# Two layers of attention and experts on one core: pair 0's scores ahead of the other queries and the values, the best keys behind its maximum, and each gathered tile split between ACT and DVE

## The chip, the cores and the metric

The kernel runs on one core of a Trainium2 chip. The metric is the device time of one execution in microseconds. Before the change three runs took 1065.91, 1067.25 and 1068.90 us, with a median of 1067.25; a profiled execution of the same kernel took 1066.29.

## What is computed

The input x has 256 tokens of 1024 features, all in fp32. A first block (attention with a causal mask, a pooling mixer, gates, an FFN with a convolution) is not touched by the change. Then come two layers (`DEPTH_2 = 2`), each of which does this:

```python
mix = hybrid_mixer(x, ...)                  # MLA and DSA side by side, then w_o
x = layer_norm(ALPHA * x + mix, ...)
ffn = grouped_moe(x, ...)                   # 16 experts, 2 for each token
x = layer_norm(ALPHA * x + ffn, ...)
```

The mixer projects x once and hands the parts to two groups of 8 heads. MLA norms a query latent of 384 and a key latent of 256, multiplies them up to queries, keys and values, and does a causal softmax. DSA has an index that picks the keys:

```python
def mla_group(...):
    q = (rms_norm(qa, q_norm_g) @ w_q_up).reshape(B, T, 8, 64 + 32)   # 32 of them rotated
    c_kv = rms_norm(kva, kv_norm_g)
    k_nope, v = c_kv @ w_uk, c_kv @ w_uv
    p = softmax(causal(q k^T * scale));  out = p @ v

def dsa_group(...):
    score = sum_h relu(iq_h ik^T * 32 ** -0.5) * iw_h      # causal
    _, sel = lax.top_k(score, n_keep)                      # n_keep = 64 of 256 keys
    s = q k_sel^T * scale - slopes * dist;  out = softmax(s) @ v_sel
```

In the MoE each token goes to two of 16 experts (two from one group of four); each expert is silu(x w_gate) * (x w_up), weighted, times w_down.

## The kernel before

T is 256 tokens, in two tiles of 128. PE multiplies in fp32 by parts: a high and a low half of each operand, and three matmuls (`mm3`, L76). `split` (L96) makes the halves: ACT copies the high one, DVE subtracts for the low one (`lo_of`, L86). So the lines L74 (every matmul), L96 and L86 are helpers' lines, and the tile names tell what is what.

A scheduler orders the instructions of each engine, by priority in program order and by costs. An engine runs its list strictly in that order. `tc.issue_after(i)` adds an edge: what is issued within it comes after instruction i on the same engine. Buffers come from pools, and a buffer's release is a wait for whoever takes it next. PSUM has two: "A" (four tiles of one bank, [128, 512] fp32) and "H" (two tiles of two banks, [128, 2, 512], for the scores `sc`). Weights go through a ring in SBUF, and for the experts through the freed buffers of the attention too; SP issues their DMAs in order, and each waits for its buffer.

In `layer` the projections come first (`proj`), and between them `index_scores`, which adds up the index heads' scores in `score`, [128, 384]: queries 0 to 127 against 128 keys, queries 128 to 255 against 256 keys. Then:

- `latent_stats` (L952 to L955): sums of squares on PE, a square root on ACT, and on DVE the reciprocal `rn`.
- `keys`: PE multiplies `knp`; `key_row` (L960) transposes rn into `prk` on PE and DVE copies it (`at`, L961); DVE multiplies both into `kx` (L975).
- `queries(g)` for the four pairs of heads: splits of `qu`, 18 matmuls into `qp`, and DVE's product with the rotation into `qx` (L1001).
- `values_`: split of `uv`, 12 matmuls into `vps`, copied by ACT.
- `mla_pair(j)`, j = 0 to 3: scores `sc` from kx and qx, the causal mask, then `softmax_heads` (L385): DVE's maximum (L390, two instructions) and scale (L394), four exponentials on ACT (L397), DVE's reciprocal (L400) and product (L402) to the normalised `P`, six transposes on PE (L406), copied half by ACT (L409) and half by DVE (L411), the matmuls with the values, and the halves oh and ol.
- `best_keys` (L934 to L939): eight rounds, each with DVE's eight largest (`MAX`, L936) and a replacement of these in `score` (`MATCH_REPLACE`, L937), for both parts of `score`; then the mask `selm` (L938, L939).
- Projections 11 and 12, and `wo_prep`: splits of w_o, issued after `first`, the normalisation (L402) of pair 0.
- `dsa_pair(j)`: scores, slopes, `selm` as a mask matmul, `softmax_heads` again, and w_o.

In the expert part `gather(q)` (L1194) fetches the tokens of four experts by matmul: four tiles `pg` of one bank, [128, 2, 256], each holding two of the eight feature blocks. `affine` (L1101 on ACT, L1103 on DVE) applies the norm's gain and bias on the way to `xg`, which `gate_up` reads for `gu`. The tiles b = 0 and 2 leave by ACT, 1 and 3 by DVE. `gather(2)` and `gather(3)` stand among the copies of an earlier expert pair's output `y` (ACT's copy L1323, DVE's low half L86), which `combine` adds up into `sum`. The weight DMAs of the experts are issued by `Experts.pump` (L733 to L757).

Of the kernel before, what the change touches and what calls it, by code (L numbers as in the profile page):

```python
# [11 lines left out]
F32R = mybir.dt.float32r  # L12
# [3 lines left out]
ALU = mybir.AluOpType  # L16
AX = mybir.AxisListType
# [17 lines left out]
def body(tc, a, out, dbg=None, upto=None):  # L35
# [17 lines left out]
    def act(name, dt=F32, shape=(128, KD, T)):  # L53
        return wp.tile(list(shape), dt, tag="act", name=name, bufs=10)
# [330 lines left out]
    def softmax_heads(S, n_, scale, nscale, values, hi, lo):  # L385

        m = sm[:, n_ % 4].rearrange("p f (h t) -> p f h t", t=2)
        P, PT = (v[:, 0:768].rearrange("p (h c) -> p h c", h=2) for v in pair_of(pp8("P")))
        for tt, (c, n) in enumerate(SPAN):
            ve.tensor_reduce(out=m[:, 0, :, tt], in_=S[:, :, c:c + n], axis=AX.X, op=ALU.max)  # L390
        if isinstance(scale, float):
            ve.tensor_scalar(m[:, 1], m[:, 0], nscale, None, op0=ALU.mult)
        else:
            ve.tensor_tensor(out=m[:, 1], in0=m[:, 0], in1=nscale[:, None, :].to_broadcast([128, 2, 2]), op=ALU.mult)  # L394
        for tt, (c, n) in enumerate(SPAN):
            for i in range(2):
                se.activation(P[:, i, c:c + n], S[:, i, c:c + n], AF.Exp,  # L397
                              scale=scale if isinstance(scale, float) else scale[:, tt:tt + 1],
                              bias=m[:, 1, i, tt:tt + 1], accum_out=m[:, 2, i, tt:tt + 1])
        ve.reciprocal(m[:, 3], m[:, 2])  # L400
        for tt, (c, n) in enumerate(SPAN):
            done = ve.tensor_tensor(out=P[:, :, c:c + n], in0=P[:, :, c:c + n],  # L402
                                    in1=m[:, 3, :, tt:tt + 1].to_broadcast([128, 2, n]), op=ALU.mult)
        for i in range(2):
            for b in range(3):
                te.transpose(S[:, i, 128 * b:128 * b + 128], P[:, i, 128 * b:128 * b + 128], ident)  # L406
        for i in range(2):
            if i == 0:
                se.activation(PT[:, i], S[:, i, 0:384], AF.Copy)  # L409
            else:  # L410
                ve.tensor_copy(PT[:, i], S[:, i, 0:384])  # L411
        o = S[:, :, 384:512]
        for i in range(2):
            mm(o[64 * i:64 * i + 64, 0], values(0, i), PT[:, i, 0:128], True, True)
        for i in range(2):
            mm(o[64 * i:64 * i + 64, 1], values(0, i), PT[:, i, 128:256], True, False)
        for i in range(2):
            mm(o[64 * i:64 * i + 64, 1], values(1, i), PT[:, i, 256:384], False, True)
        hi, lo = (v.rearrange("p (t c) -> p t c", t=2) for v in (hi, lo))
        se.activation(hi, o, AF.Copy)  # L420
        lo_of(lo, o, hi)
        return done

    def causal(S):
        for i in range(2):
            for c in (0, 256):
                mm(S[:, i, c:c + 128], identb, at.maskb[:, c:c + 128], False, True)
# [371 lines left out]
    def layer(l, xT, xh, xl, general=False):  # L799
# [178 lines left out]
        def values_():  # L978
            uvh, uvl = split(W[f"uv{l}"].rearrange("p k f -> p (k f)"))
            for tt in range(2):  # L980
                ps = A("vps")
                for k in range(2):
                    c = slice(k * 512, k * 512 + 512)
                    t_ = slice(tt * 128, tt * 128 + 128)
                    mm(ps, nh[:, 3 + k, t_], uvh[:, c], k == 0, False)
                    mm(ps, nh[:, 3 + k, t_], uvl[:, c], False, False)
                    mm(ps, nl[:, 3 + k, t_], uvh[:, c], False, k == 1)
                se.activation(vm[:, tt], ps, AF.Copy, scale=rn[:, 2, 2 + tt:3 + tt])

        def queries(g):  # L990

            qu = W[f"qu{l}"].rearrange("p k (h c) -> p k h c", c=96)[:, :, 2 * g:2 * g + 2]
            hi, lo = (v.rearrange("p (k h) c -> p k h c", h=2) for v in split(None, (6, 128)))
            for d, c in ((slice(0, 96), slice(0, 96)), (slice(96, 128), slice(64, 96))):
                se.activation(hi[:, :, :, d], qu[:, :, :, c], AF.Copy)
                lo_of(lo[:, :, :, d], qu[:, :, :, c], hi[:, :, :, d])
            ps = A("qp", (128, 2, T))
            for i in range(2):
                for k in range(3):
                    mm3(ps[:, i], hi[:, k, i], lo[:, k, i], nh[:, k], nl[:, k], k == 0, k == 2)  # L1000
            ve.tensor_tensor(out=qx[:, 2 * g:2 * g + 2], in0=ps, in1=at.qrot[:, None, :].to_broadcast([128, 2, T]), op=ALU.mult)  # L1001

        def mla_pair(j):
            S = H("sc")
            for tt, (c, n) in enumerate(SPAN):
                for i in range(2):
                    h = 2 * j + i
                    mm(S[:, i, c:c + n], qx[:, h, tt * 128:tt * 128 + 128], kx[:, h, 0:n], tt == 0, False)
            causal(S)
            return softmax_heads(S, j, rn[:, 2], rn[:, 3, 0:2], lambda s, i: vm[:, s, (2 * j + i) * 64:(2 * j + i) * 64 + 64],  # L1010
                                 oh[:, j], ol[:, j])

# [22 lines left out]
        latent_stats()  # L1035
        keys()
        qx = act("qx")
        queries(0)
        queries(1)
        values_()  # L1040
        queries(2)
        queries(3)
        oh, ol = act("oh", F32R), act("ol", F32R)
        first = [mla_pair(j) for j in range(4)][0]
        best_keys()
        for i in range(11, 13):
            proj(i)
        if not general:
# [49 lines left out]
        def affine(dst, src, k, eng):  # L1098
            g, b = V(f"ln1g{l}", k), V(f"ln1b{l}", k)
            if eng is se:  # L1100
                se.activation(dst, src, AF.Identity, scale=g, bias=b)  # L1101
            else:
                ve.tensor_scalar(dst, src, g, b, op0=ALU.mult, op1=ALU.add)  # L1103
# [79 lines left out]
        def gather(q, bs=range(4)):  # L1183

            G = GS[q]
            if q not in XG:
                XG[q] = act("xg", shape=(128, KD, 256))
            xg = XG[q]
            for b in bs:
                pg = A("pg", (128, 2, 256))  # L1190
                for tt in range(2):
                    for i in range(2):
                        k = 2 * b + i
                        mm(pg[:, i], zh[:, tt, k], G[:, tt], tt == i == 0, False)  # L1194
                        mm(pg[:, i], zl[:, tt, k], G[:, tt], False, tt == 1)
                for i in range(2):
                    affine(xg[:, 2 * b + i], pg[:, i], 2 * b + i, (se, ve)[b % 2])

        def gate_up(p, m):
            ps = A("gu")  # L1200
# [305 lines left out]
```

## Time and profile before

| | |
|---|---|
| median of three runs | 1067.25 us (1065.91 to 1068.90) |
| the profiled execution | 1066.29 us |
| its span in the trace | 1064.2 us, mean granted clock 0.994 |
| PE busy | 1020.2 us, 96% |
| DVE / ACT / POOL busy | 50% / 40% / 7% |
| DMA | 278 GB/s over the span, 388 GB/s from 497 to 700 us |
| layer 0: attention and DSA / experts | about 397 to 470 us / 486 to 700 us |
| layer 1: MLA / experts | about 746 to 794 us / 848 to 1054 us |

The span runs from the first to the last instruction; the execution's own time adds 2.1 us around it. A row of the timeline has its start in us, its length, engine, line, operation, what is written and read, shapes and count, and in brackets the idle time before it with the instruction that ended it. A row of a window has the busy time and count of each engine, the granted clock of TensorE (1.00 is 2.4 GHz), the DMA share and GB/s.

### The profile page before, as it was taken

What the parts mean: (1) busy time and instruction counts of PE and PEld (TensorE: products, weight loads), DVE (VectorE), ACT (ScalarE), POOL (GpSimd) and SP (SyncE); (2) the same over time, 40 slices, a digit from 0 to 9 for tenths busy, and PEclk for the clock granted to TensorE, in tenths of its full rate; (3) what the DMA queues carried; (4) which work ended last, traced back from release to release, by engine and by line L of the source; (5) the groups of instructions that cost most, each with busy time, mean ns of one, the idle gap of its engine ahead of it and who ended that gap; (6) DMA issues with size and microseconds to landing.
All of it is one profiled execution on the core that took longest, in us unless ns stands there. A gap on an engine that the chain in (4) does not pass through costs nothing.

```text
span 1064.2 us, 16619 instructions
## 1 busy us (share of the span) xinstructions
PE 1020.2 (96%) x6768; PEld 729.5 (69%) x6768; DVE 529.7 (50%) x1010; ACT 424.0 (40%) x781; POOL 75.5 (7%) x80
## 2 busy tenths in 40 slices
PE   9999999999999998999999999999899999999995
PEld 7889999999999998765343434379787534343432
DVE  6775568977777679753111111158976402021103
ACT  5675548655554475541111111166554302011111
POOL 3400021000000010010000000041000200000001
PEclk9999999999999999999999999999999999999998
DMA  9943555755443244987999999975378899999994
GB/s 339 348 139 126 186 199 173 249 207 168 156 145 144 95 159 159 352 314 272 396 393 393 400 399 396 388 262 193 139 286 320 285 385 393 400 400 400 395 390 163
DMA packets 131796, 295.41 MB, mean 278 GB/s; under 512 B 6054, under 2 KB 36976, under 8 KB 125440
## 3 DMA queue, kind: packets, MB, share of 16 engines
q1 hardware_dynamic: 129936, 290.35, 74.3%
q0 software_dynamic: 1472, 3.40, 1.0%
q8 instruction: 55, 0.90, 0.3%
q10 hardware_dynamic: 304, 0.53, 0.1%
q14 instruction: 29, 0.24, 0.1%
HBM read 292.15 MB, written 2.10 MB: 277 GB/s over the span
## 4 chain that ended last, share of the span: by engine, by line
PE 78%; DVE 11%; ACT 5%; DMA 3%; issue 2%; POOL 0%; ACTq 0%; DVEq 0%; POOLq 0%; SPq 0%
PE gu L74 20%; PE up L74 12%; PE pd L74 10%; PE fm L74 7%; PE yT L74 6%; PE tm L74 4%; PE wo L74 3%; PE pg L74 3%; PE sc L74 3%; DVE hl L86 3%; PE sum L74 2%; PE prj L74 2%; ACT P L397 2%; PE sc L406 1%; ACT hl L96 1%
## 5 line engine op out<-in xcount | busy, mean ns | idle before, releaser
L74 PE MATMUL gu<-e,xg 128*64 128x512 f32 x1024 | 226.8, 595 | 1.3 <-ACT sg L1292 1.3
L74 PEld LDWEIGHTS gu<-e,xg 128*64 128x64 f32 x1024 | 71.2, 137 | 134.4 <-issue 126.8
L74 PE MATMUL up<-h2h,hl 128*128 128x256 f32 x704 | 130.5, 284 | 0.0
L74 PE MATMUL pd<-e,aT 128*64 128x512 f32 (+1 forms) x544 | 113.9, 571 | 2.3 <-ACT aT L1307 2.3
L74 PEld LDWEIGHTS up<-h2h,hl 128*128 128x128 f32 x704 | 111.5, 192 | 0.0
L74 PE MATMUL up<-h2l,hl 128*128 128x256 f32 x352 | 99.9, 284 | 0.1
L74 PEld LDWEIGHTS pd<-e,aT 128*64 128x64 f32 x544 | 37.5, 137 | 71.5 <-issue 61.4
L74 PEld LDWEIGHTS up<-h2l,hl 128*128 128x128 f32 x352 | 67.7, 192 | 0.3 <-DVE h2l L522 0.3
L1223 DVE TENSOR_REDUCE gcol<-pgt 64x1 f32<-64x2 f32 x32 | 5.0, 157 | 124.8 <-PE pgt L74 124.6
L74 PE MATMUL yT<-ac,hl 128*128 128x256 f32 x528 | 67.0, 284 | 0.1
L1298 DVE SCALAR_TENSOR_TENSOR sg<-gu,gcol,sg 128x512 f32<-128x512 f32 x16 | 12.0, 751 | 110.0 <-PE gu L74 110.0
L74 PEld LDWEIGHTS yT<-ac,hl 128*128 128x128 f32 x528 | 64.9, 192 | 0.3 <-ACT ac L642 0.3
L86 DVE TENSOR_TENSOR hl<-up,hl 128x1024 fp32r<-128x1024 f32 x44 | 53.8, 1224 | 19.5 <-ACT hl L96 19.4
L1292 ACT ACTIVATE sg<-gu 128x512 f32<-128x512 f32 x16 | 9.6, 597 | 128.0 <-PE gu L74 128.0
L96 ACT ACTIVATE hl<-up 128x1024 fp32r<-128x1024 f32 x44 | 46.1, 1051 | 33.9 <-PE up L74 28.4
L1323 ACT ACTIVATE y<-pd 128x512 fp32r<-128x512 f32 (+1 forms) x34 | 18.7, 570 | 94.3 <-PE pd L74 81.0
L86 DVE TENSOR_TENSOR y<-pd,y 128x512 fp32r<-128x512 f32 (+1 forms) x34 | 21.6, 654 | 66.4 <-ACT y L1323 66.4
L1307 ACT ACTIVATE aT<-pact 128x512 f32<-128x512 f32 x16 | 9.6, 597 | 110.2 <-PE pact L1305 110.2
L74 PE MATMUL fm<-hh,hl 128*128 128x256 f32 x256 | 49.2, 288 | 0.9 <-ACT vu L323 0.9
L1103 DVE TENSOR_SCALAR xg<-pg,vec 128x256 f32<-128x256 f32 x32 | 15.9, 539 | 60.8 <-PE pg L74 59.2
L86 DVE TENSOR_TENSOR hl<-in,hl 128x1024 fp32r<-128x1024 f32 x32 | 38.6, 1219 | 11.0 <-ACT hl L96 10.8
L74 PE MATMUL prj<-xhn,hl 128*128 128x256 f32 x208 | 40.6, 292 | 1.7 <-POOL hl L86 1.0
(356 smaller groups left out, 2022.9 us busy)
## 6 DMA issues: line engine op xcount, KB each, us to landing
e<-in_w_up_dram SPq DMA_DIRECT2D x48, 1024.0 KB, 13.2
e<-in_w_down_dram SPq DMA_DIRECT2D x48, 1024.0 KB, 13.6
e<-in_w_gate_dram SPq DMA_DIRECT2D x40, 1024.0 KB, 14.7
e<-in_w_gate_dram SPq DMA_DIRECT2D x48, 512.0 KB, 10.8
up<-in_w_up_dram SPq DMA_DIRECT2D x22, 1024.0 KB, 5.1
e<-in_w_up_dram SPq DMA_DIRECT2D x32, 512.0 KB, 10.8
in<-in_w_in_dram SPq DMA_DIRECT2D x15, 1024.0 KB, 17.6
down<-in_w_down_dram SPq DMA_DIRECT2D x11, 1024.0 KB, 4.9
```

The lines of the kernel that those rows point to most:

```text
L74: return te.matmul(o, lhsT=l, rhs=r, start=start, stop=stop, skip_group_check=True)
L86: return (eng or ve).tensor_tensor(out=dst, in0=src, in1=hi.bitcast(F32), op=ALU.subtract)
L96: se.activation(hi, raw, AF.Copy, scale=scale)
L397: se.activation(P[:, i, c:c + n], S[:, i, c:c + n], AF.Exp, scale=scale if isinstance(scale, float) else scale[:, tt:tt + 1], bias=m[:, 1, ...
L406: te.transpose(S[:, i, 128 * b:128 * b + 128], P[:, i, 128 * b:128 * b + 128], ident)
L1103: ve.tensor_scalar(dst, src, g, b, op0=ALU.mult, op1=ALU.add)
L1223: ve.tensor_reduce(out=gcol[r, p:p + 1], in_=pt[r, x:x + 17:16], axis=AX.X, op=ALU.add)
L1292: se.activation(sg, psg, AF.Silu)
L1298: ve.scalar_tensor_tensor(out=sg, in0=psu, scalar=gcol[:, p:p + 1], in1=sg, op0=ALU.mult, op1=ALU.mult)
L1307: se.activation(aT, pt, AF.Copy)
L1323: se.activation(h_, ps, AF.Copy)
```

## The change

Three edits. In `layer` the scores of pair 0 are issued behind queries(0), its softmax behind the values, pair 1's scores behind queries(2), its softmax behind queries(3), and pairs 2 and 3 as before. `best_keys` is issued after `most`, the second of pair 0's two maxima, on DVE. In `gather` the two feature blocks of each tile leave PSUM one by ACT and one by DVE, in place of whole tiles by turns. The lines of the changed kernel behind the first place are 11 higher (L1101 and L1103 are L1112 and L1114).

```diff
-            ve.tensor_reduce(out=m[:, 0, :, tt], in_=S[:, :, c:c + n], axis=AX.X, op=ALU.max)
+            most = ve.tensor_reduce(out=m[:, 0, :, tt], in_=S[:, :, c:c + n], axis=AX.X, op=ALU.max)
...
-        return done
+        return done, most
...
-        def mla_pair(j):
+        def mla_scores(j):
             S = H("sc")
...
             causal(S)
+            return S
+
+        def mla_pair(j, S):
             return softmax_heads(S, j, rn[:, 2], rn[:, 3, 0:2], lambda s, i: vm[:, s, (2 * j + i) * 64:(2 * j + i) * 64 + 64],
                                  oh[:, j], ol[:, j])
...
         qx = act("qx")
+        oh, ol = act("oh", F32R), act("ol", F32R)
+
         queries(0)
+        S = mla_scores(0)
         queries(1)
         values_()
+        first, most = mla_pair(0, S)
         queries(2)
+        S = mla_scores(1)
         queries(3)
-        oh, ol = act("oh", F32R), act("ol", F32R)
-        first = [mla_pair(j) for j in range(4)][0]
-        best_keys()
+        mla_pair(1, S)
+        for j in (2, 3):
+            mla_pair(j, mla_scores(j))
+
+        with tc.issue_after(most.ins):
+            best_keys()
...
-                    affine(xg[:, 2 * b + i], pg[:, i], 2 * b + i, (se, ve)[b % 2])
+                    affine(xg[:, 2 * b + i], pg[:, i], 2 * b + i, (se, ve)[i])
```

What the engines' lists become. DVE around the first maximum of layer 0, before (`hl<-wb` is the low half of a projection's weights):

```order
L1001 TENSOR_TENSOR qx<-qp,at 128x512
L937 MATCH_REPLACE score<-m_3882,score 128x256
L937 MATCH_REPLACE score<-m_3882,score 128x128
L936 MAX m_3882<-score 128x8
L86 TENSOR_TENSOR hl<-wb_3904,hl 128x1024
L1001 TENSOR_TENSOR qx<-qp,at 128x512
L937 MATCH_REPLACE score<-m_3882,score 128x256
L390 TENSOR_REDUCE sm<-sc 128x2 x2
L938 TENSOR_SCALAR score<-score 128x384
L394 TENSOR_TENSOR sm<-sm,rn 128x4
L939 TENSOR_TENSOR selm<-score,at 128x384
```

All eight rounds stand ahead of the maximum there, three of them ahead of the key row's copy (L961) as well. DVE at the same place in the changed kernel, from the qx of pairs 0 and 1 on:

```order
L1001 TENSOR_TENSOR qx<-qp,at 128x512 x2
L86 TENSOR_TENSOR hl<-qu_3902,hl 128x6x32
L86 TENSOR_TENSOR hl<-wb_3904,hl 128x1024
L390 TENSOR_REDUCE sm<-sc 128x2 x2
L936 MAX m_3882<-score 128x8
L394 TENSOR_TENSOR sm<-sm,rn 128x4
L936 MAX m_3882<-score 128x8
L937 MATCH_REPLACE score<-m_3882,score 128x128
L937 MATCH_REPLACE score<-m_3882,score 128x256
```

The maximum now stands behind two of the four qx and ahead of every round. Three rounds follow it before pair 0's reciprocal, the others stand between the steps of pairs 0 to 2, and selm comes here:

```order
L402 TENSOR_TENSOR P<-P,sm 128x2x128
L402 TENSOR_TENSOR P<-P,sm 128x2x256
L390 TENSOR_REDUCE sm<-sc 128x2 x2
L938 TENSOR_SCALAR score<-score 128x384
L394 TENSOR_TENSOR sm<-sm,rn 128x4
L411 COPY P<-sc 128x384
L939 TENSOR_TENSOR selm<-score,at 128x384
L86 TENSOR_TENSOR dq_3917<-prj,dq_3917 128x256 x2
L86 TENSOR_TENSOR hl<-wo_3906,hl 128x1024
L86 TENSOR_TENSOR ol<-sc,oh 128x256
L400 RECIPROCAL sm<-sm 128x4
```

The first two rows are pair 2's product, the next the maximum of pair 3, the last pair 3's reciprocal. On PE the scores of pair 0 go between the first and the following matmuls of the values; with + what is new at this place:

```order
 L74 MATMUL qp<-nh,hl 128x256
 L74 MATMUL vps<-hl,nh 128x512 x2
+L74 MATMUL sc<-kx,qx 128x128 x2
+L74 MATMUL sc<-kx,qx 128x256 x2
+L74 LDWEIGHTS identb
+L74 MATMUL sc<-at,identb 128x128
```

Ten matmuls of the values, queries(2) and pair 1's scores follow before pair 0's transposes. The third place is the gather of a later quarter of the experts (q = 2) in layer 0, DVE before, with the semaphores that each waits for (Activation is ACT):

```order
L86 TENSOR_TENSOR y<-pd,y 128x512 [waits Activation_49] x2
L1103 TENSOR_SCALAR xg<-pg,vec 128x256 [waits DMAHW4_49,DMAHW0_49,PE_49]
L1103 TENSOR_SCALAR xg<-pg,vec 128x256
L86 TENSOR_TENSOR y<-pd,y 128x512 [waits DMAHW7_49,DMAHW3_49,Activation_49]
L86 TENSOR_TENSOR y<-pd,y 128x512 [waits Activation_49]
L1103 TENSOR_SCALAR xg<-pg,vec 128x256 [waits PE_49]
L1103 TENSOR_SCALAR xg<-pg,vec 128x256
```

And in the changed kernel:

```order
L86 TENSOR_TENSOR y<-pd,y 128x512 [waits Activation_49] x2
L86 TENSOR_TENSOR y<-pd,y 128x512 [waits DMAHW6_49,DMAHW7_49,DMAHW3_49,Activation_49]
L86 TENSOR_TENSOR y<-pd,y 128x512 [waits Activation_49]
L1114 TENSOR_SCALAR xg<-pg,vec 128x256 [waits DMAHW4_49,DMAHW0_49,Activation_49]
L1114 TENSOR_SCALAR xg<-pg,vec 128x256 [waits Activation_49] x3
```

The four low halves of y stand ahead of all of DVE's xg, and each of DVE's xg waits for ACT, where it waited for PE.

## Rows read from the trace of the kernel before

**Rows 1.** The page, busy time of PE, share of the span and instructions.
```profile
PE 1020.2 (96%) x6768; PEld 729.5 (69%) x6768; DVE 529.7 (50%) x1010; ACT 424.0 (40%) x781; POOL 75.5 (7%) x80
```

**Rows 2.** Windows: busy time of each engine, granted clock, DMA share, GB/s.
```profile
412.00:427.00 15.00, 12.17 (x104) 11.10 (x103) 14.07 (x38) 7.77 (x23) 0.00 (x0) 1.00 0.50 177
497.00:700.00 203.00, 197.47 (x965) 81.62 (x963) 28.00 (x61) 30.94 (x57) 2.03 (x1) 1.00 1.04 388
```

**Rows 3.** PE's waits, layer 0's MLA, then DSA: total us, times, longest.
```profile
PE sc L406 <- DVE P L402: 2.4, 1, 2.4
PE prj L74 <- DVE hl L86: 0.4, 1, 0.4
PE qp L74 <- DVE at L961: 0.4, 1, 0.4
...
PE sc L406 <- DVE P L402: 0.8, 2, 0.4
PE sc L74 <- DVE P L411: 0.3, 1, 0.3
```

**Rows 4.** PE's waits, layer 1's MLA.
```profile
PE sc L406 <- DVE P L402: 2.6, 1, 2.6
PE prk L960 <- DVE rn L952: 1.2, 1, 1.2
PE prj L74 <- DVE hl L86: 0.3, 1, 0.3
```

**Rows 5.** Timeline of DVE in layer 0.
```profile
399.67 0.16 DVE L952 RECIPROCAL rn<-rn 128x4 f32<-128x4 f32 x1
...
403.45 2.80 DVE L975 TENSOR_TENSOR kx<-knp,at 64x512 f32<-64x512 f32 x4
406.28 1.29 DVE L1001 TENSOR_TENSOR qx<-qp,at 128x512 f32<-128x512 f32 x2
...
409.04 0.08 DVE L937 MATCH_VALUE_LOAD score<-m,score 128x8 f32 x1
...
410.22 0.08 DVE L937 MATCH_VALUE_LOAD score<-m,score 128x8 f32 x1
...
417.05 1.01 DVE L390 TENSOR_REDUCE sm<-sc 128x2 f32<-128x256 f32 x2
...
418.36 0.56 DVE L939 TENSOR_TENSOR selm<-score,at 128x384 bf16<-128x384 f32 x1
...
420.82 1.02 DVE L402 TENSOR_TENSOR P<-P,sm 128x256 f32<-128x256 f32 x2
```

**Rows 6.** Timeline of PE in layer 0: pair 0's scores, and selm's first use.
```profile
412.22 1.48 PE L74 MATMUL sc<-kx,qx 128*128 128x128 f32 x8
...
443.75 0.49 PE L74 MATMUL sc<-selm,identb 128*128 128x384 bf16 x2
```

**Rows 7.** Window in layer 1, behind PE's wait for P.
```profile
771.00:775.00 4.00, 3.79 (x20) 3.83 (x21) 3.22 (x8) 3.07 (x9) 0.00 (x0) 0.57 0.46 176
```

**Rows 8.** A later gather: PE's waits from 497 to 700; timelines of DVE, ACT, PE.
```profile
PE pg L74 <- DVE xg L1103: 1.7, 2, 0.9
...
593.65 0.99 DVE L1103 TENSOR_SCALAR xg<-pg,vec 128x256 f32<-128x256 f32 x2 [10.27 <-PE pg L74]
594.57 1.28 DVE L86 TENSOR_TENSOR y<-pd,y 128x512 fp32r<-128x512 f32 x2
...
591.54 1.09 ACT L1323 ACTIVATE y<-pd 128x512 fp32r<-128x512 f32 x2 [7.86 <-PE pd L74]
...
594.70 0.39 PE L74 MATMUL pg<-G,zh 128*128 128x256 f32 x1 [0.86 <-DVE xg L1103]
```

**Rows 9.** Layer 1's last weights: issue, KB and us to landing, and first use.
```profile
1029.90 0.37 SPq L751 DMA_DIRECT2D e<-in_w_down_dram  x1
...
e<-in_w_down_dram SPq DMA_DIRECT2D x1, 768.0 KB, 13.2
...
1042.60 2.37 PE L74 MATMUL pd<-e,aT 128*64 128x512 f32 x10
```

## The prediction

> **What bounds the kernel now.** I read the page first: PE is busy for 1020.2 us of a span of 1064.2 [rows 1]. A change that takes no matmul away can only fill the 44 us in which PE idles, so the question is how much of that lies at the places that the change touches, and what would fill it instead. The windows come next [rows 2]: in layer 0's attention, from 412 to 427, PE loses 2.8 of 15 us while DVE works for 14.07; in the expert stretch PE is at 197.47 of 203 and the DMA share is 1.04, with 388 GB/s. So the attention is bound by PE with DVE close behind it, and the expert stretch by PE and the weight stream together. PE's waits name the releasers. Layer 0: 2.4 us for the first pair's normalised P (L402), 0.4 for the rotated key row (L961), 0.4 for a projection's low half, and 1.1 us in the DSA pairs [rows 3]. Layer 1: 2.6, 1.2 for rn, and 0.3 [rows 4]. All are waits for DVE.
>
> Why is DVE late? Its timeline shows that best_keys, which nobody needs yet, stands in front of what PE waits for [rows 5]. Two rounds of best_keys start 1.18 us apart (409.04 and 410.22). The order places three of eight rounds before the key row and the other five before the first maximum (L390), which runs at 417.05, although pair 0's scores were started at 412.22 and take 1.48 [rows 6]. selm, the product of best_keys, is done at 418.9, and PE first uses it at 443.75: 25 us of slack spent at the wrong moment.
>
> **The first part: scores and softmax of pair 0 moved up, best_keys behind its maximum.** No arithmetic is added or taken away. Walking the new DVE order with the durations of rows 5: the key rounds that stood before the reciprocal of rn are gone, so it runs at about 397.6 for 399.67, and the key row, kx (2.80) and the first qx (0.65) end at about 404.9. PE needs no wait before queries(1) (0.38 saved), starts the scores of pair 0 at about 405.2 (412.22 before) and ends them at 406.7. The maximum takes 1.0, to 407.9. From a maximum's end to its P's multiplication 2.8 us went by (418.06 to 420.82), the scale and four exponentials; with a copy of vps between them on ACT I put their end at 411.1. Meanwhile DVE does three rounds, 3 x 1.18 = 3.5 us, and is free at about 411.7. The reciprocal, the qx of queries(2) (0.65) and the two multiplications (1.02) put the normalised P at 413.4. PE has ten vps matmuls, queries(2) and the scores of pair 1 in between, some 6.5 us, and comes for P at about 413.0: **a wait of 0.3 for 2.43**. The same walk through pairs 1 to 3 gives waits of 0.35 before pair 1's values, 0.1 three times, and 0.4 before pair 3's transposes, because the remaining rounds stand between them. With the key row's and the projection's small waits that makes about 1.4 us, for 3.2 before: gain 1.8. In the DSA pairs I estimate 0.75 for 1.1, since their first maximum can come some 8 us earlier: 0.35. **Layer 0: 2.15.**
>
> Layer 1 has the same order with old waits of 2.6 + 1.2 + 0.3 = 4.1; the 1.2 for rn falls away for the reason given. 4.1 - 1.4 + 0.35 = **3.05.**
>
> What is late next is selm: by the order it now comes after pair 2's copy (L411), at about 429.4, while PE reaches its first use at about 433.5. So 4 us of margin remain. Behind the ordering edge on `most` nothing queues but best_keys' own instructions. wo_prep hangs on pair 0's normalisation, which now comes 8 us earlier; DVE does its low halves in the gaps, and they are in my walk. On SP the same weight transfers stand in nearly the same order; the first expert gates wait for the low half of wb, which DVE reaches 7 us earlier, so nothing there comes later.
>
> **The clock.** In layer 1 the 2.6 us wait is followed by a granted clock below full: 0.57 over the four microseconds from 771, most of them at half speed, 1.2 GHz [rows 7]. It costs 4 x 0.43 = 1.7 us. In layer 0 the 2.43 us wait cost none (1.00 throughout [rows 2]). With waits below 0.5 us I expect no drop: **1.7 us**. Bounds: nothing, if some longer wait stays, and 1.7.
>
> **The gathers.** "At once" is not what the order shows: each DVE half waits for ACT's half of the same tile (the section on the change). Before, the third tile waited 0.86 us for DVE's two instructions on the second tile, and the low half of an expert's output stood behind them [rows 8]; two such waits per layer make 1.7. In the new order the low halves come first and the third tile's buffer is freed by them. They need only ACT's y (591.54 to 592.6), so they end at about 593.4, when PE comes: the wait goes, 2 x 0.86 = 1.7 per layer. ACT has four halves of a gather before and after, and DVE four of 0.5: no engine has more work. The first and second gathers have no such wait; their second half is ready 0.1 us later and used a matmul group later: nothing.
>
> The PSUM page of the Trainium skill ("PSUM — Partial Sum Buffer", section "PSUM bank collisions raise a hardware error") says that two engines must not touch one bank on the same partitions together, reads included. The tile is one bank, so by that rule ACT and DVE take turns, and the waits in the order agree; if the turns were the whole story the gather would gain nothing, which is in rival C.
>
> How much of 1.7 can be kept? The last weight transfers are the check: issued at 1029.90, the fourth quarter lands 13.2 us later, at 1043.1, and PE first needs it at the eleventh matmul from 1042.60, 10 x 0.215 later at 1044.75 [rows 9]. The stream runs without a gap through the stretch, so PE may come 1.65 us earlier and no more. I take 1.65 for each layer, as layer 0's stream has the same shape: **3.3.** The attention's gains are not capped so, since the stream's start shifts with them.
>
> **Sum.** 2.15 + 3.05 + 1.7 + 3.3 = 10.2. Against the profiled execution's 1066.3 that is **1056.1 us.** That execution lies 0.96 below the median of the three runs (1067.25) and inside their spread of 3.0; I leave the forecast unshifted. Bounds: with every one of these waits gone, 3.2 + 1.1 + 4.1 + 1.1 + 1.7 + 3.4 = 14.6, that is 1051.7.
>
> **The rivals.** B: *PE waits as long as before, elsewhere.* The last four rounds now stand inside pairs 1 to 3, between maximum and normalisation; if each pair stalls 0.8 us on P, 3 us per layer are back, the drop of the clock stays, and only the gathers gain: 1066.3 - 3.3 = 1063.0. For it: DVE was busy for 14.07 of 15 us. Against: selm's slack was 25 us.
>
> C: *The weight stream binds the expert stretch, or ACT's and DVE's turns cost what the order saves.* Then the 3.3 fall away: 1059.4. For it: a DMA share of 1.04 without a pause. Against: the 1.65 us of slack at its end. The DMA page of the Trainium skill ("DMA: Bandwidth & Descriptors", section "Where 436 GB/s comes from") has the HBM side bind at about 358 GB/s for a core, by which the stream would be at its limit already and this rival likely. The trace shows 388 GB/s in that stretch, above it, so the measurement decides and the chance stays moderate.
>
> D: *selm comes too late, slower than before.* If the scheduled rounds slip behind the softmaxes of all four pairs, best_keys' 8 x 1.18 = 9.4 us come after them and PE waits 9.4 - 4.1 = 5.3 us per layer at the first DSA mask. So long an idle stretch also lowers the clock in both layers, 1.7 more than now. 1066.3 + 10.6 + 1.7 - 3.3 = 1075.3. It turns slower than before once selm slips by some 6 us per layer. For it: DVE is full. Against: by the order selm stands before pair 3's normalisation.
>
> E: B and C together, about 1066.
>
> **How the numbers follow.** Forecast 0.60, B 0.16, C 0.14, D 0.07, E 0.03. About 0.3%, 3.2 us, is what a measurement of this kernel can tell from no change; faster means below 1064.0. B's 1063.0 lies just inside, and I give half of it to either side. Faster 0.60 + 0.14 + 0.08 = 0.82; same 0.08 + 0.03 = 0.11; slower 0.07. The range goes from the bound 1051.7 to B's 1063.0, each moved out by half the runs' spread (1.5): 1050.2 to 1064.5. It leaves out D, E and a little of B.
>
> **What would show it.** Right: pair 0's maximum within 2 us of 407; its transposes waiting under 0.5 us; no wait of PE's for rn in layer 1 and a granted clock of 1.00 around 772; selm ready before PE needs it; no wait of pg for xg near 594, and the first use of the last weights not waiting for a DMA. Wrong: a wait of over 0.8 us before transposes of pairs 1 to 3 (B), waits of gu or pd for a DMA that grow by what pg lost (C), the first selm matmul waiting for L939 (D).

## The result and the profile after

The changed kernel takes **1059.93 us** (median of 6 runs, 1058.86 to 1062.59) where the kernel before took 1067.25 in the same comparison: a ratio of **0.9927** (95% interval 0.9916 to 0.9939). The forecast was 1056.1 in a range of 1050.2 to 1064.5. The sign and most of the reasons hold, but of the forecast 10.2 us only 7.3 came by the medians, and 6.85 between the two profiled executions.

The profiled execution took 1059.44 us, with a span of 1057.3 for 1064.2. Its busy time of PE and three windows, to be held against [rows 1, 2, 7]:

```profile
PE 1019.1 (96%) x6768; PEld 730.1 (69%) x6768; DVE 531.4 (50%) x1010; ACT 425.6 (40%) x781; POOL 76.6 (7%) x80
...
412.00:427.00 15.00, 12.81 (x113) 11.53 (x112) 14.82 (x56) 9.47 (x26) 0.00 (x0) 1.00 0.29 109
497.00:700.00 203.00, 197.91 (x971) 83.14 (x967) 29.30 (x61) 31.40 (x56) 2.90 (x2) 1.00 1.04 389
771.00:775.00 4.00, 4.00 (x37) 3.63 (x34) 4.00 (x15) 3.57 (x11) 0.00 (x0) 1.00 0.00 0
```

PE executes the same 6768 matmuls; the gain is idle time and clock. In layer 1 the clock no longer falls around 771. In layer 0 PE still loses 2.2 of 15 us.

Where the 6.9 us of the span (1064.2 less 1057.3) lie shows when the same matmuls start in both traces (`ssq`: the sums of squares ahead of the keys; `gu`: the first expert matmul; `sum`: the last wait for the statistics):

| stage | before, from - to | after | change | predicted |
|---|---|---|---|---|
| ahead of layer 0's `ssq` | 395.51 | 395.68 | +0.17 | 0 |
| layer 0, attention and routing: `ssq` to `gu` | 395.51 - 487.12 | 395.68 - 486.50 | -0.79 | -2.15 |
| layer 0, experts, up to layer 1's `ssq` | 487.12 - 744.16 | 486.50 - 743.32 | -0.22 | -1.65 |
| layer 1, attention and routing | 744.16 - 838.54 | 743.32 - 833.03 | -4.67 | -4.75 |
| layer 1, experts, up to the last `sum` | 838.54 - 1052.36 | 833.03 - 1045.59 | -1.26 | -1.65 |
| the rest | 11.8 | 11.7 | -0.1 | 0 |

So layer 1's attention came as forecast, and layer 0 missed both times. PE's waits after, from 390 to 430 (first line), 430 to 480 and 740 to 794, answer to [rows 3, 4]:

```profile
PE sc L406 <- DVE P L402: 2.2, 1, 2.2
...
PE sc L406 <- DVE P L402: 1.0, 3, 0.5
...
PE sc L406 <- DVE P L402: 1.8, 3, 1.1
```

The waits for rn, for the key row and for the projection's half are gone in both layers. One wait of 2.2 is left in layer 0's first three pairs, at pair 0's first transpose, where I had 0.3; the other waits that I walked (0.35, 0.1, 0.4) are down to one of 0.25, ahead of pair 3's transposes. In layer 1 the two are 1.09 and 0.25. DVE's timeline in layer 0 says why (these are the steps of [rows 5]):

```profile
397.76 0.17 DVE L952 RECIPROCAL rn<-rn 128x4 f32<-128x4 f32 x1
...
401.48 2.80 DVE L975 TENSOR_TENSOR kx<-knp,at 64x512 f32<-64x512 f32 x4
404.31 1.29 DVE L1001 TENSOR_TENSOR qx<-qp,at 128x512 f32<-128x512 f32 x2
...
405.79 3.41 DVE L86 TENSOR_TENSOR hl<-wb,hl 128x1024 fp32r<-128x1024 f32 x1
409.12 1.01 DVE L390 TENSOR_REDUCE sm<-sc 128x2 f32<-128x256 f32 x2
...
410.25 0.14 DVE L394 TENSOR_TENSOR sm<-sm,rn 128x4 f32<-128x4 f32 x1
...
414.31 1.01 DVE L402 TENSOR_TENSOR P<-P,sm 128x256 f32<-128x256 f32 x2
...
430.84 0.55 DVE L939 TENSOR_TENSOR selm<-score,at 128x384 bf16<-128x384 f32 x1
```

Up to the qx the walk was right to 0.2 us. Then one subtraction of 1.22 us takes **3.41**. It stands still while POOL makes the low half of the next projection's weights, and ends 1.1 us after POOL does. In layer 1 DVE is first and POOL stands still instead (3.46 for 2.37), and DVE's next instruction that reads two tiles in SBUF, the scale of 0.14 us, takes 1.22. POOL in layer 0, then DVE and POOL in layer 1:

```profile
405.74 2.37 POOL L86 TENSOR_TENSOR hl<-wb,hl 128x1024 fp32r<-128x1024 f32 x1 [10.93 <-ACT hl L96]
```

```profile
753.43 1.22 DVE L86 TENSOR_TENSOR hl<-wb,hl 128x1024 fp32r<-128x1024 f32 x1
754.57 1.02 DVE L390 TENSOR_REDUCE sm<-sc 128x2 f32<-128x256 f32 x2
755.50 0.28 DVE L936 MAX8 m<-score 128x8 f32<-128x128 f32 x1
755.70 1.22 DVE L394 TENSOR_TENSOR sm<-sm,rn 128x4 f32<-128x4 f32 x1
...
753.45 3.46 POOL L86 TENSOR_TENSOR hl<-wb,hl 128x1024 fp32r<-128x1024 f32 x1 [10.65 <-issue]
```

The maximum (from PSUM) and MAX8 (one tile in SBUF) run beside POOL at their usual lengths. PE: pair 0's scores as early as walked, the wait, and selm's first use, 4 us behind selm, so rival D has no part in this:

```profile
405.06 1.58 PE L74 MATMUL sc<-kx,qx 128*128 128x128 f32 x8
...
414.86 0.30 PE L406 MATMUL sc<-ident,P 128*128 128x128 f32 x1 [2.19 <-DVE P L402]
...
435.65 0.33 PE L74 MATMUL sc<-selm,identb 128*128 128x384 bf16 x1
```

In the later gather, DVE then PE (compare [rows 8]), the low halves of y are done at 593.24, the third tile starts without a wait, and DVE's half waits for ACT's, 0.34 us that nobody misses:

```profile
591.95 1.29 DVE L86 TENSOR_TENSOR y<-pd,y 128x512 fp32r<-128x512 f32 x2 [9.20 <-ACT y L1334]
593.16 0.54 DVE L1114 TENSOR_SCALAR xg<-pg,vec 128x256 f32<-128x256 f32 x1
594.03 0.54 DVE L1114 TENSOR_SCALAR xg<-pg,vec 128x256 f32<-128x256 f32 x1 [0.34 <-ACT xg L1112]
...
593.46 0.28 PE L74 MATMUL pg<-G,zh 128*128 128x256 f32 x1
```

That is 1.1 us a gather. Layer 0 gives it back at its end. ACT, then PE, in the last 16 us of its experts, and last the down matmuls of the kernel before:

```profile
695.88 1.15 ACT L96 ACTIVATE hl<-wi,behind 128x1024 fp32r<-128x1024 f32 x1 [2.04 <-DMA wi<-in_w_in_dram]
696.93 0.36 ACT L1334 ACTIVATE y<-pd 128x256 fp32r<-128x256 f32 x1
697.87 1.15 ACT L96 ACTIVATE hl<-wi,behind 128x1024 fp32r<-128x1024 f32 x1 [0.57 <-DMA wi<-in_w_in_dram]
698.93 0.36 ACT L1334 ACTIVATE y<-pd 128x256 fp32r<-128x256 f32 x1
```

```profile
688.78 6.15 PE L74 MATMUL pd<-e,aT 128*64 128x512 f32 x32
...
700.23 0.48 PE L74 MATMUL sum<-y,GT 128*128 128x256 f32 x2 [0.75 <-DVE s L780]
```

```profile
691.22 5.38 PE L74 MATMUL pd<-e,aT 128*64 128x512 f32 x32
```

The next layer's first weights (`wi`) stand behind the last expert's in SP's queue, and their split stands ahead of ACT's last two copies of y. So the end of this stretch is the landing of `wi`, whatever PE saved. In layer 1, which has no next layer, only the stall within the down matmuls is left (5.77 for 5.38): a matmul starts at 1037.55, right behind the landing of the last weights' fourth quarter (issued at 1024.36, landed 13.1 us later).

### The profile page after: what moved, and what is told of

The parts are those of the page before. It is cut to its first block, busy times and chain, and to the rows that moved or that the text cites. A ratio compares the mean times of both kernels' runs of the same rounds, so it can differ in the third digit from the quotient of the medians.

```text
span 1057.3 us, 16626 instructions
## 1 busy us (share of the span) xinstructions
PE 1019.1 (96%) x6768; PEld 730.1 (69%) x6768; DVE 531.4 (50%) x1010; ACT 425.6 (40%) x781; POOL 76.6 (7%) x80
## 4 chain that ended last, share of the span: by engine, by line
PE 85%; DVE 8%; ACT 4%; DMA 1%; issue 1%; POOL 1%; ACTq 0%; DVEq 0%; POOLq 0%
PE gu L74 21%; PE up L74 12%; PE pd L74 11%; PE fm L74 7%; PE prj L74 6%; PE yT L74 6%; PE tm L74 4%; PE wo L74 3%; PE pg L74 3%; PE sum L74 3%; PE sc L74 2%; DVE hl L86 2%; PE sc L406 1%; DMA wa<-in_w_in_dram 1%; ACT P L397 1%
## 5 line engine op out<-in xcount | busy, mean ns | idle before, releaser
L74 PE MATMUL wo<-hl,oh 128*128 128x512 f32 x128 | 43.9, 409 | 0.0
L74 PE MATMUL sum<-y,GT 128*128 128x512 f32 (+1 forms) x136 | 38.8, 404 | 3.0 <-ACT y L1334 1.6
```

The lines of the kernel that those rows point to most:

```text
L74: return te.matmul(o, lhsT=l, rhs=r, start=start, stop=stop, skip_group_check=True)
```

## The experiments

The ratio to the kernel before, beside its interval, is from the runs on the same chip. The stage columns come from the profiled executions, as above (change against before's profile; "drop" marks a granted clock of half speed for 3.4 us, which costs 1.7 us, within the stage; before has one in layer 1's attention, so a kernel without one there shows -1.7 from the clock alone).

| kernel | us | ratio (95%) | attn. 0 | experts 0 | attn. 1 | experts 1 |
|---|---|---|---|---|---|---|
| changed | 1059.93 | 0.9927 (0.9916-0.9939) | -0.79 | -0.22 | -4.67 | -1.26 |
| gather_only | 1064.88 | 0.9973 (0.9963-0.9983) | 0.00 | -0.33 | -1.86 | -1.24 |
| attn_only | 1063.73 | 0.9967 (0.9957-0.9978) | +0.69 drop | +0.31 | -4.69 | +0.47 |
| scores_only | 1067.55 | 0.9998 (0.9983-1.0012) | +0.54 | +0.31 | -1.43 | +2.15 drop |
| keys_only | 1064.40 | 0.9977 (0.9962-0.9991) | -0.77 | +0.33 | -3.55 | +0.75 |
| no_pool | 1056.64 | 0.9900 (0.9883-0.9917) | -2.94 | -0.21 | -5.74 | -0.41 drop |
| pool_twice | 1062.83 | 0.9959 (0.9946-0.9972) | +1.82 drop | -0.25 drop | -4.66 | -0.79 |
| after_less | 1058.27 | 0.9916 (0.9899-0.9932) | -0.79 | -0.24 drop | -4.67 | -2.21 |
| before_less | 1066.98 | 0.9997 (0.9984-1.0010) | +0.03 | -0.10 | -0.12 drop | +0.04 |
| y_first | 1065.44 | 0.9992 (0.9971-1.0014) | +0.03 | -0.39 | -0.30 drop | -0.72 |
| thirds | 1055.48 | 0.9888 (0.9872-0.9903) | -2.94 | +0.09 | -5.71 | -2.06 |
| tail1 | 1055.69 | 0.9886 (0.9872-0.9901) | -2.96 | -1.14 | -5.72 | -1.92 |
| late_scores | 1061.45 | 0.9937 (0.9924-0.9950) | +0.31 drop | -0.14 | -3.51 | -1.47 |

The stages ahead of layer 0 differ by -0.3 to +2.0 us between these executions; where they are over 0.9 (gather_only, scores_only, after_less, tail1) a drop lies near 176.

**The three edits apart.** gather_only is the kernel before with the last hunk; attn_only is the changed kernel without it.

> The kernel before with the gather's edit alone. Theory 1 (layer 0's expert stretch ends with the weight stream, because the next layer's first weights stand behind the last expert's and ACT waits for them ahead of its last copies): layer 0 gains 0.2 us, layer 1 1.3, so about 1065.7 for 1067.25. Rival (the prediction's sum): 1.65 in each layer, 1063.9. Rival (turns of ACT and DVE cost what the order saves): no change. In all cases no wait of pg for xg is left in the later gathers.

> The changed kernel with the gather as before: both edits of the attention. Theory 1: layer 0 gains 0.8, layer 1 4.7, so about 1061.7. Rival (the three edits do not add up, since the weight stream or another wait takes the attention's gain back in the expert stretch): over 1063. The waits of PE for P stay at 2.2 us in layer 0 and 1.1 at most in layer 1.

The gather's edit alone gives 0.27%, 2.9 us, more than theory 1's 1.5 and less than the rival's 3.3, so the time does not decide. The stages do: 0.33 and 1.24 in the experts, as theory 1 said by place. The rest of that profile's gain lies in layer 1's attention, which the edit does not touch: PE waits 2.6 us for P there as before, and the clock does not fall. Windows of gather_only, behind that wait and in the first block:

```profile
176.00:181.00 5.00, 4.89 (x29) 4.92 (x30) 4.40 (x5) 3.69 (x5) 0.00 (x0) 0.66 0.25 70
771.00:775.00 4.00, 2.40 (x21) 2.43 (x22) 3.15 (x8) 4.00 (x15) 0.00 (x0) 1.00 0.78 286
```

attn_only gave 3.5 us where theory 1 had 5.5. Its layer 1 is right; in layer 0 the wait of 2.2 is followed by a fall of the clock that the changed kernel's profile does not have. Another 0.8 us is lost in the experts (+0.31 and +0.47), where theory 1 had nothing: as the rival said, another wait takes it, one for `sg` that the part on the prediction describes. The fall of the clock:

```profile
416.00:420.00 4.00, 4.00 (x27) 3.45 (x26) 2.91 (x14) 2.50 (x9) 0.00 (x0) 0.57 0.09 36
```

**Which of the attention's two edits.** Both leave the gather as before.

```diff
# scores_only, from attn_only
-        with tc.issue_after(most.ins):
-            best_keys()
+        best_keys()
# keys_only, from the kernel before (the edits that hand out `most` are left out)
...
-        first = [mla_pair(j) for j in range(4)][0]
-        best_keys()
+        first, most = [mla_pair(j) for j in range(4)][0]
+        with tc.issue_after(most.ins):
+            best_keys()
```

> As attn_only, but best_keys without the ordering edge: only the scores and softmaxes are moved. Theory 1 (where the key rounds stand decides): the order puts three rounds ahead of the key row again and four more between pair 0's maximum and its P, so PE waits over 4 us for P in each layer, the granted clock falls behind it, and the kernel is slower than before: 1069 to 1073. Rival (the early scores are what helps): 1062 to 1065.

> The kernel before with best_keys behind pair 0's maximum and nothing else. Theory 1: the rounds leave the path of rn, the key row and the first maximum; PE has a whole projection between the scores and the first transposes, so the wait for P of 2.4 and 2.6 us goes, and the clock's fall in layer 1 with it: 1058 to 1061 if selm comes in time, at least as good as attn_only. Rival (both edits are needed): 1064 or more, with a wait for P of over 1 us. Rival (selm, which the order puts behind pair 3's copy, is late): PE waits at the first DSA mask, 1063 or more.

scores_only gains nothing and loses nothing. Theory 1's 4 us at P did not come: the wait there is 1.3, but others took its place, and their sum is the 3.2 us of before. PE's waits in layer 0's MLA:

```profile
PE sc L406 <- DVE P L402: 1.3, 1, 1.3
PE sc L74 <- DVE qx L1001: 1.2, 1, 1.2
PE qp L74 <- DVE at L961: 0.4, 1, 0.4
PE sc L74 <- DVE P L411: 0.3, 1, 0.3
```

So the scores by themselves move the wait about, and the keys' place is needed. It is not enough either: keys_only still waits 1.7 us for pair 0's P in both layers. Theory 1 was wrong there, the rival "both edits are needed" right. In time keys_only and attn_only cannot be told apart (0.9977 and 0.9967). By stages, keys_only gains in layer 0's attention as much as the changed kernel (0.77 and 0.79); the early scores add 1.1 us in layer 1 (4.67 for 3.55). The rows of keys_only, PE's wait and DVE ahead of it, say what it waits for now: not for DVE's rounds but for PE's scores, which come last.

```profile
PE sc L406 <- DVE P L402: 1.9, 2, 1.7
...
413.23 1.02 DVE L390 TENSOR_REDUCE sm<-sc 128x2 f32<-128x256 f32 x2 [0.85 <-PE sc L74]
```

**POOL and DVE.**

```diff
# no_pool, from the changed kernel (i is the projection)
-                eng = ge if l and i < 5 or i == 12 else ve
+                eng = ge if l and i < 5 else ve
# pool_twice, from the changed kernel, behind the split
+                if i == 12:
+                    lo_of(WS[i][1], wcol(C0[n] + 128 * j, 128), WS[i][0], ge)
```

> The changed kernel with the low half of projection 12's weights on DVE in place of POOL; DVE's order is the same but for this one, which comes ahead of pair 2's reciprocal. Theory 1 (in layer 0 DVE's subtraction of wb stands still while POOL's runs, 3.41 us for 1.22, and that is PE's 2.2 us at pair 0's P): the instruction takes 1.22, the wait falls under 0.6 in layer 0; in layer 1 the scale L394 takes 0.14 for 1.22 and the wait of 1.1 falls under 0.5. Some 2 to 2.5 us faster than the changed kernel, 1057.5. Rival (DVE was late for another reason, its input for one): the duration stays at 3.4 and the time within 0.5 us of 1059.9. Rival (DVE is full, 1.22 us more per layer come out as a wait later): 1059 to 1061.

> The changed kernel with POOL's subtraction for projection 12's weights done twice, same operands. Theory 1 (an instruction of DVE that reads two tiles in SBUF and one of POOL take turns, each for its whole length): in layer 0 POOL's second run goes behind DVE's wb, to about 411.5, and the scale L394 (two SBUF operands, 0.14 us) waits for it: 1.2 us more wait for P. In layer 1 the second run meets only rounds and PSUM reads, and costs nothing. About 1061. MAX, MATCH_REPLACE, the maxima and the qx products (one SBUF operand) keep their durations. Rival (no such exclusion): 1059.9 and no duration of DVE changed.

no_pool is 3.3 us faster than the changed kernel by the medians (2.9 by the ratios), more than expected: DVE's subtraction takes 1.22, and PE does not wait at all in either layer's MLA. DVE in no_pool:

```profile
405.72 1.22 DVE L86 TENSOR_TENSOR hl<-wb,hl 128x1024 fp32r<-128x1024 f32 x1
406.85 1.02 DVE L390 TENSOR_REDUCE sm<-sc 128x2 f32<-128x256 f32 x2
...
412.04 1.02 DVE L402 TENSOR_TENSOR P<-P,sm 128x256 f32<-128x256 f32 x2
```

The product is done at 413.06, where my walk had 413.4. In pool_twice the doubled instruction does what theory 1 said: the scale takes 1.22, and PE waits 3.3 us for 2.2. POOL, DVE and PE's wait in layer 0:

```profile
405.39 5.71 POOL L86 TENSOR_TENSOR hl<-wb,hl 128x1024 fp32r<-128x1024 f32 x2 [10.93 <-ACT hl L96]
...
409.90 1.22 DVE L394 TENSOR_TENSOR sm<-sm,rn 128x4 f32<-128x4 f32 x1
...
PE sc L406 <- DVE P L402: 3.5, 2, 3.3
```

Its time, 1062.83, is 1.8 above the expected 1061; its profile has two drops of the clock, one behind this wait, which I had not counted. So the effect of the doubled instruction is read from the lengths and the wait, not from the time.

**The weight stream.** One expert's gate weights, 2 MB a layer, are not loaded in after_less and before_less; that expert computes with another's.

```diff
+                if p == 5 and m == 0 and e == 1:
+                    t = self.last[0]
...
+                    continue
```

> The changed kernel without the load of one expert's gate weights in each layer (2 MB; expert 11 computes with expert 10's). Theory 1 (the weight stream ends the expert stretch): the stream ends 5 us earlier, so the 0.78 us of stall in layer 0's last down matmuls, the 0.75 at the sums behind it and the 0.41 in layer 1 go: 1058.0. Rival (PE's order ends it): 1059.9.

> The kernel before with the same 2 MB left out of the load in each layer. Theory 1 (the kernel before had 1 to 1.7 us of slack at the stream's end): within 0.5 us of 1067.25, so that changed and unchanged kernel lie 9 us apart without the stream's limit where they lie 7.3 apart with it. Rival (the stream already bound the kernel before): faster by 1 us or more.

Both as theory 1 had them: 1058.27, and no change for the kernel before. In after_less layer 0's stalls at the end are gone and layer 1's experts gain 2.2 us instead of 1.26; in layer 0 a drop of the clock ate 1.7 of it in the profiled execution. The stream did not bind the kernel before, and binds the changed one. That rests on the traces: in time after_less and the changed kernel overlap (0.9899 to 0.9932, and 0.9916 to 0.9939).

thirds and tail1 build on no_pool and go at the end of layer 0 itself.

```diff
# thirds, from no_pool
-                        for c in (slice(0, 768), slice(768, D)):
+                        for c in (slice(0, 512), slice(512, 768), slice(768, D)):
# tail1, from thirds
-                    after(2, y[:, 1, 511:512].bitcast(F32))
                     combine(7, (0,))
...
                     rows_out(1, t, 2)
+                    after(2, y[:, 1, 1023:1024].bitcast(F32))
```

> As no_pool, with the last expert's down weights loaded as columns 0 to 511, 512 to 767, 768 to 1023 in place of 0 to 767 and the rest, so that what the first matmuls need lands some 2.6 us earlier. Theory 1 (layer 0 ends with the next layer's first weights, behind all of these in the queue): the stall of 0.8 us in layer 0's last down matmuls goes but comes back at the sums, so only layer 1 gains, 0.4: about 1056.3. Rival (the late down weights alone cost layer 0 its gain): 1.2 us or more under no_pool's 1056.6.

> As thirds, and the split of the next layer's first weights on ACT held back behind the last low half of y, so that ACT's last two copies of y do not stand behind a wait for those weights. Theory 1: the sums no longer wait for the statistics (0.75 us), PE does not wait in layer 0's last down matmuls, and layer 0's expert stretch keeps what its gathers gain: 1.6 us under no_pool, 1055. Rival (the next layer's projections then wait for the split instead): no faster than thirds, with a wait of prj for hl of over 1 us at layer 1's start.

thirds shows the shift that theory 1 foresaw: the down matmuls take 5.38 again, and PE waits at the sums instead, since `wi` lands no earlier. Layer 0's experts gain nothing (+0.09), and layer 1's gain 2.06 where the changed kernel had 1.26. PE in thirds:

```profile
685.77 5.38 PE L74 MATMUL pd<-e,aT 128*64 128x512 f32 x32
...
694.98 0.96 PE L74 MATMUL sum<-y,GT 128*128 128x256 f32 x4 [0.82 <-ACT y L1334]
...
697.92 0.48 PE L74 MATMUL sum<-y,GT 128*128 128x256 f32 x2 [1.10 <-DVE s L780]
```

tail1 takes the split out of ACT's way. The sums no longer wait, and layer 0's experts gain 1.14. The other 1.0 comes back as a wait that I had not named: both splits, 2.19 us, now stand on ACT ahead of the norm that PE needs next. ACT, then PE, in tail1:

```profile
696.46 2.19 ACT L96 ACTIVATE hl<-wi,behind 128x1024 fp32r<-128x1024 f32 x2 [0.68 <-DVE behind L110]
...
701.36 2.08 PE L772 MATMUL pt<-ident,z 128*128 128x128 f32 x16 [0.79 <-ACT z L795]
```

In time thirds and tail1 cannot be told apart (1055.48 and 1055.69), as tail1's rival had it, though the wait stands elsewhere. Both beat the changed kernel by 4 us, most of it no_pool's; from no_pool itself their intervals do not part them.

**What the gather's gain is.** y_first leaves the tiles to ACT and DVE by turns and only puts DVE's part behind the last low half of y.

```diff
+                    if b % 2 and "lo" in LAST:
+                        with tc.issue_after(LAST["lo"].ins):
+                            affine(xg[:, 2 * b + i], pg[:, i], 2 * b + i, ve)
...
-                    lo = lo_of(l_, ps, h_)
+                    lo = LAST["lo"] = lo_of(l_, ps, h_)
```

> The kernel before, gathered tiles leaving by ACT and DVE in turn as before, but in the later gathers DVE's part issued behind the last low half of y. Theory 1 (the gather's gain is DVE's order, y's low halves freeing PSUM tiles for the third gathered tile, not the split of each tile): no wait of pg for xg, about 1.1 us off each later gather, and the same time as with the gather's edit alone, 0.9973 of before within 0.0012. Rival (two engines for each tile are what helps): pg waits as long or longer, 0.999 to 1.001 of before.

No wait of pg for xg is left and each later gather is 1.1 us shorter, as with the split. In time the runs do not resolve it (0.9992, interval up to 1.0014): one of the twelve took 1078.07 us at a granted clock of 0.945, while the median, 1065.44, is 0.9980 of before's 1067.56. The trace does resolve it at the gathers. Of the gain there, 0.39 and 0.72 are left at the ends of the layers, for gather_only's 0.33 and 1.24; in layer 1 a down matmul waits 0.42 us for its weights. So the split of the tiles is not what removed the waits; the order of DVE's list is.

**The early scores, once POOL is out of the way.** late_scores is keys_only with the gather's hunk and no_pool's line.

> As no_pool without the first edit: keys behind the maximum, gather, and no POOL in the attention, but the scores of all pairs behind the queries and values as before. Theory 1 (behind the maximum, P takes ACT and DVE longer than PE's one projection lasts, so the early scores are needed): the wait for P stays at 1.7 us in each layer, since DVE waits for PE's scores there and not for POOL; 3 to 4 us slower than no_pool, about 1060.2. Rival (with POOL out of the way the early scores are worth nothing): 1056.6 within 1 us.

The wait of 1.7 stays in both layers, and the kernel is 4.8 us slower than no_pool by the medians (3.9 by the ratios). Each profile has one drop of the clock, in different stages; without its drop, late_scores loses 1.5 us in layer 0's attention and 2.2 in layer 1's. All of the first two edits is needed.

## Why the prediction was right or wrong

- **The bound and the rearrangement: right.** The rounds off the path, the scores at 405.06 for a walked 405.2, the waits for rn and the key row gone, selm 4 us ahead of its use. scores_only shows that the keys' place is needed, keys_only that the early scores are, in layer 1, and late_scores that with POOL out of the way they are in both. Of the signs that I named, the maximum ran at 409.12, just outside 2 us of 407, and pair 0's transposes waited 2.2 and 1.1 us for under 0.5; B's sign, over 0.8 before pairs 1 to 3, did not come.
- **Layer 1's attention, 3.05 + 1.7: right in size**, 4.67, in part by luck. PE's waits at the places that I summed, MLA and DSA, fell from 5.4 to 2.1 (2.6 + 0.8 + 1.2 + 0.3 + 0.3 + 0.2 before, P alone after); with the clock's 1.7 that makes 5.0, and 4.67 came. Of the MLA's waits 1.34 are left, for a walked 1.4, but not where I had them: 1.09 for pair 0's P (walked 0.3), because the scale took 1.22 for 0.14 behind POOL, and 0.25 at the other pairs (walked 1.1). Two errors of opposite sign cancelled. no_pool, without the first, gains 5.74 here.
- **Layer 0's attention, 2.15: wrong, 0.79.** The step that failed is "The maximum takes 1.0, to 407.9": the walk priced each DVE instruction by its usual length, and with them the low half of wb ahead of the maximum. POOL's subtraction, at the same place in time, cost 2.2 (3.41 for 1.22), so the maximum ended at 410.1. Of the 1.36 us that are missing, that wait is 1.9 (2.19 for 0.3); 0.85 came back, because the other pairs waited 0.25 for a walked 1.1. The rest is no wait: PE is busy for 85.25 us in this stage for 84.86 before, with the same matmuls, and why stays open. no_pool, which differs from the changed kernel only in the engine of that subtraction, gains 2.94 there, more than the walked 2.15, since the walked waits of the other pairs are gone too. The trace of before had shown it, in rows that I did not read: a low half of 0.34 us that took 1.63, while POOL ran.

```profile
407.49 1.63 DVE L86 TENSOR_TENSOR hl<-qu,hl 128x192 fp32r<-128x192 f32 x1
```

```profile
406.50 2.40 POOL L86 TENSOR_TENSOR hl<-wb,hl 128x1024 fp32r<-128x1024 f32 x1 [11.85 <-ACT hl L96]
```

- **The gathers, 1.65 in each layer: right in how, wrong in size.** The waits went, and by y's low halves (y_first); each later gather gained 1.1, some 2.1 a layer for my 1.7, and the ends of the layers kept less. What failed is "as layer 0's stream has the same shape": behind layer 0's last expert weights come the next layer's, and ACT waits for them ahead of PE's last inputs. In layer 1 the cap of 1.65 was mis-sized: I let the eleventh down matmul be the first that needs the fourth quarter, but the one that starts behind its landing in the changed kernel is the tenth. Before, the tenth starts at 1044.4, 1.3 us behind the landing of 1043.1. So 0.22 and 1.26. That is rival C's first half in layer 0; its second half, that turns of ACT and DVE eat the gain, did not come: DVE's 0.34 us of waiting costs nothing.
- **A cost that I did not have**: in both layers the changed kernel waits 1.0 us for a product on DVE (sg) at about 581, where it waited 0.27, because two `sum` matmuls that stood ahead of it on PE now stand behind it. PE is 0.4 us later behind it in each layer, but at the layer's end it costs next to nothing while the weights set that end: gather_only, which does not have this wait, keeps 0.33 and 1.24 for 0.22 and 1.26. In attn_only, which has no gain to be capped, it shows as +0.31 and +0.47. no_pool, thirds and tail1 do not have it.
- **The clock, 1.7 gained: came in this profile, but by the luck of the execution as much as by the edit.** The same wait of 2.6 us was followed by a fall in before, before_less and y_first, and by none in gather_only; the wait of 2.2 us by one in attn_only and by none in the changed kernel and after_less. Why it falls in one execution and not in another stays open. It also blurs every comparison of times by up to 1.7 us for each place: of the changed kernel's six runs three, at a mean granted clock of 0.996, took 1058.86 to 1059.44 us, and three, at 0.992 and 0.993, took 1060.42 to 1062.59. Of the 6.9 us between the profiles the edits' own share is 5.2, an estimate: 6.9 less one drop.

The sum by stages: 2.15 + 4.75 + 3.3 = 10.2 forecast, 0.79 + 4.67 + 1.48 = 6.94 in the profile. That the measured 1059.93 lies near rival C's 1059.4 is chance: C dropped all of the gathers' 3.3 and kept the attention's 6.9, where 1.48 and 5.46 came.

## What to carry to other kernels

When you walk an engine's new order by hand, look not only at what each instruction took but at what other engines ran beside it: an instruction that is longer than its like can mark a shared resource, and moving the order moves the collision. A low-priority job on an idle engine is not free: here 2.4 us on POOL cost DVE, and so PE, 2.2. And where a sum comes out right, compare its terms one by one: here layer 1's total hid two errors. And before you credit a stretch that ends with a stream of transfers, follow the queue one transfer past the last that the stretch itself needs.

## What the runs showed of the hardware

DVE's instructions that read two tiles in SBUF and POOL's that read SBUF take turns, each for its whole length: 3.41 us for 1.22 where POOL came first, 3.46 for 2.37 where DVE did, and 1.22 for 0.14 on a tiny one. DVE's reads of PSUM and its MAX8 and MATCH_REPLACE, with one tile in SBUF, kept theirs. The Trainium skill says so in "SBUF — State Buffer", section "Who interferes with whom": a DVE instruction with two inputs in SBUF contends with a GpSimd instruction that reads SBUF, the ports that they share are an exclusive lock, and the order of issue decides which of them blocks. The lengths above agree; by that rule the walk would have had the 2.2 us.

TensorE's granted clock falls to half, 1.2 GHz, for 3.4 us at a time, 1.7 us lost, at one or two of some five places (about 176, 416 or 431, 508, 771, and 850 to 859) in one execution of these kernels and at none in another (the last 7 to 10 us of every span, behind the last wait for the statistics, are at half speed too). Ahead of these falls PE had waited 0.2 us at 176, 1.7 to 3.3 at 416, 431 and 771, and 0.95 and 0.69 at 508 and 850 to 859; up to 2.6 us the same waits stand in executions without the fall as well. In layer 0's experts such a drop cost almost nothing by the stage's end (pool_twice -0.25, the changed kernel -0.22 without one), because the weight stream ends that stretch.
